# Four of seven Strassen products in two matmuls where a call also has plain units, with tighter room for prefetch and folded scales

## The chip, the cores and the metric

The kernel runs on one core of a Trainium2 chip. The metric is the device time of one execution in microseconds (us), as the median of several runs. Beside it stands one profiled execution, from which every duration below is read. "PE" is TensorE's matmul stream, "PEld" its weight loads (which overlap it), "DVE" VectorE, "ACT" ScalarE, "POOL" GpSimd and "SP" SyncE, which here only issues DMAs.

## The reference

One layer of a decoder trunk over 512 tokens with width 2048, all in float32:

```python
h = rmsnorm(x, attn_norm_g)
u, v_sgu, q, k, v_att, g_a, g_b = split(h @ w_in)          # 2048 -> 9216 columns
y_a = gelu(u) * chunked_spatial_gating(rmsnorm(gelu(v_sgu)))  # 8 groups, chunks of 128
y_b = stick_breaking_attention(rmsnorm(q, q_norm_g), rmsnorm(k, k_norm_g), v_att)  # 8 heads of 128
merged = sigmoid(g_a) * (y_a @ w_up_a) + sigmoid(g_b) * (y_b @ w_up_b)
x = x + merged @ w_o
hid = rmsnorm(x, ffn_norm_g) @ w_ffn_in                    # 2048 -> 2 x 5632
x = x + (silu(gate) * up) @ w_ffn_out                      # 5632 -> 2048
x = x + sigmoid(rmsnorm(x, ple_norm_g) @ w_ple_gate) * (p @ w_ple)
```

The attention's scores are scaled by 1/sqrt(128). All RMS norms add 1e-6 to the mean square.

## The kernel before

**Numbers in two halves.** A float32 value is split into a high half, rounded to the type that the matmul takes at full rate (fp32r), and a low half, the rest. A product of two such values needs high x high, high x low and low x high. `mm3` (lines 275 to 279) issues these as three matmuls: the high weight against the high data, the high weight against the low data, the low weight against the high data. The high half is made by an ACT copy, the low half by a DVE subtraction: `split_into` (L272, L273) for the data, `Weights.steps` (L346, L343) for the weights. A split operand is called a form; its halves lie in the arena `parts`, its raw block in the arena `wholes`.

**Units and calls.** One unit is a 256 x 256 block of a weight against 256 rows and 512 tokens of data. A call (`pair`) makes 256 output columns for all tokens and goes over the units of the inner dimension. A unit is either plain ("P": four block products, each an `mm3` over 512 tokens) or Strassen ("S", in Winograd's form: seven products of 128 x 128 blocks against 256 columns, for which sums of data blocks and of weight blocks are prepared). Two neighbouring units of one kind share one weight transfer and are worked product by product together. The strings `OUT`, `PASSES` and `GATE` tell the kinds: w_o and the gate have "SSSSSSPP", FFN-out goes in three passes over its inner dimension with "SSSSSSPP", "SSSSSSP" and "SSSPPPP". The calls of w_in and FFN-in are all "S".

**Single and doubled products.** The data's high and low halves lie side by side. A doubled product (`twice`, L686) therefore runs the high weight once over 512 columns, high and low halves together, into a whole PSUM bank, and the low weight over 256 columns into that bank's first half: two matmuls and two weight loads in place of three, with the same 768 columns. The two halves of the bank have to be added later. The number of doubled products of a call is its argument `doubled`: five in w_in, seven in FFN-in. Where a call has plain units too, the kernel before sets it to zero, and all seven products go through `mm3`.

**Banks and mixing.** There are six rotating PSUM banks ("ps") and two more ("small"). An undoubled call holds four banks: "a" and "q" (two products each in halves), "z" and "y". With plain units, these run into z and y as well. While the last Strassen units run, `mix` takes one step after each product: ACT copies a and q out (L697), DVE adds them up (L700). At the end `rest` subtracts from y and adds to z on DVE (L779). `mix_doubled` (L729, L732) does the like for the all-Strassen calls, with each doubled bank's first half copied by ACT and its second half added by DVE.

**Order.** The program text is written by Python, and a scheduler orders each engine's instructions; `in_turn` and `tick` tie some of them to places among the units. A tick comes about once a plain unit and twice a pair of Strassen units. At a tick the first form waiting in `builds` is made if its room can be had, one of the first three is fetched, and sums of late forms are made. A late form is one whose raw block is fetched ahead of its place in `parts`; its four sums (`sums_of`, L531) go into two extra blocks. Whether room can be had is asked by `fits` (L163 on), which tries the takes, a spare block of 1024 that the caller adds, and one more of 1024 that it adds itself. `keep_for` decides at the end of a call whether the block just finished is kept as the next form's raw block. In w_o, the next layer's forms may be fetched from the second last call on.

**Queues.** SP issues nearly all transfers, in one order: weights (L326, L328, L330), blocks of x, of the hidden layer and of partial sums (L513), and stores. POOL issues the weight sums, which add in flight (L350). At the start SP issues both halves of p, then the weight of the first product (`w_ple[0]`, L326), then x and the gains (L887); five small matmuls on zeros run ahead (L881). The squares of x for the first norm are made as each block of x is scaled (`norm1.add`, L935, L939).

**Scales.** q is multiplied by its RMS factor and, in a DVE operation on that factor (L1052), by 1/sqrt(128), then by its gain on ACT while it is copied out (L1057). k is multiplied by its gain in an ACT pass of its own over 1024 columns (L1065).

## Time and profile before

| | us |
|---|---|
| median of 3 runs | 2702.89 (2701.41 to 2705.18) |
| profiled execution | 2700.52 |
| its span, first to last instruction | 2698.7 |
| PE busy | 2664.3 |
| PEld busy | 2369.2 |
| DVE busy | 2201.6 |
| ACT busy | 1368.7 |
| POOL busy | 388.7 |

The granted TensorE clock is 0.997 of full speed over the span. 536.20 MB move over the DMA queues, 199 GB/s in the mean. Busy times are unions over the span and overlap each other; a matmul's row covers its way through the array, so neighbouring matmuls overlap too, and the rate of the stream is read from starts or from the length of a stretch and the count in it. L-numbers are lines of the kernel before. By the rows of the trace, w_in and its attention run to about 845 us, the two up-projections to 1025, w_o to 1180, FFN-in from 1188 to 2054, the three FFN-out passes to 2534 with bounds near 2235 and 2390, and the gate to the end.

### The profile page before, as it was taken

The page shows a single profiled execution, that of the slowest core. Times are in us where ns is not written, and L with a number is a line of the kernel's source. Part 1 is how long each engine was busy: PE and PEld are TensorE (multiplying, and loading weights), DVE is VectorE, ACT ScalarE, POOL GpSimd, SP SyncE. Part 2 cuts the span into 40 slices and gives each one's busy share as a digit, 9 for nine tenths or more (in the row PEclk, how much of TensorE's full clock was granted, in tenths as well). Part 3 has the DMA queues.
Part 4 walks back from the last instruction along what each step waited for, and adds up shares of the span by engine and source line. Part 5 has one row for each costly group of instructions (what it writes and reads, how often), then busy time and mean ns, then how long its engine had stood idle before and what let it go on. Part 6 is the DMA issues. An engine that isn't in the chain of part 4 may idle for free.

```text
span 2698.7 us, 43910 instructions
## 1 busy us (share of the span) xinstructions
PE 2664.3 (99%) x16244; PEld 2369.2 (88%) x16244; DVE 2201.6 (82%) x3750; ACT 1368.7 (51%) x2143; POOL 388.7 (14%) x450
## 2 busy tenths in 40 slices
PE   9999999999999999999999999999999999999999
PEld 7888888888988889988888888888888999989898
DVE  7787878787887668788999898989899668788876
ACT  7655656565554334465444444444445344444643
POOL 0212121212220001101111111111110101101010
PEclk9999999999999999999999999999999999999999
DMA  6676677767776458767887878877877768878784
GB/s 214 168 181 167 177 177 177 178 175 193 175 186 213 133 151 251 208 204 194 222 212 196 208 201 202 205 203 196 213 196 214 188 175 248 229 246 242 251 251 128
DMA packets 287879, 536.20 MB, mean 199 GB/s; under 512 B 25648, under 2 KB 140720, under 8 KB 287664
## 3 DMA queue, kind: packets, MB, share of 16 engines
q1 hardware_dynamic: 228016, 426.55, 49.5%
q0 software_dynamic: 59648, 106.85, 24.0%
q8 instruction: 127, 2.08, 0.3%
q14 instruction: 88, 0.72, 0.1%
HBM read 486.11 MB, written 47.19 MB: 198 GB/s over the span
## 4 chain that ended last, share of the span: by engine, by line
PE 82%; DVE 9%; DMA 3%; ACT 3%; issue 2%; POOL 1%; SPq 0%; DVEq 0%; ACTq 0%; POOLq 0%
PE ps L686 37%; PE ps L279 13%; PE ps L277 13%; PE ps L278 13%; PE small L686 4%; DVE wlo L343 3%; DVE out L732 1%; DVE parts L273 1%; ACT whi L346 1%; DMA wholes<-w_in 1%; DVE wholes L531 1%; DVE wholes L732 1%; DMA wholes<-x 1%; PE small L1126 1%; PE small L1084 1%
## 5 line engine op out<-in xcount | busy, mean ns | idle before, releaser
L346 ACT ACTIVATE whi<-wholes 128x512 fp32r<-128x512 f32 (+3 forms) x937 | 854.9, 938 | 834.2 <-PE ps L278 318.3
L686 PE MATMUL ps<-parts,whi 128*128 128x512 f32 x3384 | 1129.3, 398 | 4.2 <-DVE p L732 2.9
L343 DVE TENSOR_TENSOR wlo<-wholes,whi 128x512 fp32r<-128x512 f32 (+3 forms) x937 | 972.8, 1072 | 63.6 <-ACT whi L346 61.6
L277 PE MATMUL ps<-parts,whi 128*128 128x256 f32 (+1 forms) x2784 | 869.5, 315 | 8.9 <-ACT whi L346 4.1
L278 PE MATMUL ps<-parts,whi 128*128 128x256 f32 (+1 forms) x2749 | 869.5, 317 | 2.9 <-DVE parts L273 2.9
L279 PE MATMUL ps<-parts,wlo 128*128 128x256 f32 (+1 forms) x2749 | 867.4, 317 | 1.7 <-DVE wlo L343 1.7
L686 PEld LDWEIGHTS ps<-parts,wlo 128*128 128x128 f32 x3384 | 635.8, 188 | 142.3 <-DVE wlo L343 1.2
L686 PE MATMUL ps<-parts,wlo 128*128 128x256 f32 x3384 | 668.3, 279 | 0.8 <-DVE wlo L343 0.8
L277 PEld LDWEIGHTS ps<-parts,whi 128*128 128x128 f32 x2784 | 529.7, 190 | 49.4 <-ACT whi L346 7.1
L278 PEld LDWEIGHTS ps<-parts,whi 128*128 128x128 f32 x2749 | 523.3, 190 | 40.3 <-DVE parts L273 3.5
L279 PEld LDWEIGHTS ps<-parts,wlo 128*128 128x128 f32 x2749 | 523.3, 190 | 35.5 <-DVE wlo L343 3.0
L686 PEld LDWEIGHTS ps<-parts,whi 128*128 128x128 f32 x3384 | 543.8, 189 | 12.1 <-DVE p L732 4.4
L362 DVE TENSOR_TENSOR wholes<-wholes 128x256 f32<-128x256 f32 (+1 forms) x810 | 339.6, 419 | 35.4 <-issue 11.8
L350 POOL DMA_DIRECT2D wholes<-w_ffn_in x172 | 147.8, 859 | 740.1 <-DMA wholes<-w_ffn_in 209.1
L732 DVE TENSOR_TENSOR out<-out,ps 128x256 f32<-128x256 f32 x373 | 152.1, 419 | 124.9 <-ACT out L729 114.9
L350 POOL DMA_DIRECT2D wholes<-w_in x132 | 115.7, 876 | 596.6 <-DMA wholes<-w_in 195.0
L273 DVE TENSOR_TENSOR parts<-wholes,parts 128x1024 fp32r<-128x1024 f32 (+4 forms) x142 | 130.3, 932 | 10.2 <-ACT parts L272 10.0
L686 PE MATMUL small<-parts,whi 128*128 128x512 f32 x344 | 136.0, 395 | 0.0
L272 ACT ACTIVATE parts<-wholes 128x1024 fp32r<-128x1024 f32 (+4 forms) x142 | 111.8, 821 | 34.8 <-DMA wholes<-hid 13.5
L1403 ACT ACTIVATE out<-out 128x512 f32<-128x512 f32 x44 | 27.9, 633 | 190.0 <-DVE out L1402 190.0
L350 POOL DMA_DIRECT2D wholes<-w_ffn_out x56 | 50.9, 908 | 403.3 <-DMA wholes<-w_ffn_out 119.5
L700 DVE TENSOR_TENSOR out<-out 128x256 f32<-128x256 f32 x36 | 15.2, 424 | 102.5 <-ACT out L697 99.1
(129 smaller groups left out, 1673.5 us busy)
## 6 DMA issues: line engine op xcount, KB each, us to landing
wholes<-w_ffn_in SPq DMA_DIRECT2D x172, 384.0 KB, 5.6
wholes<-w_in SPq DMA_DIRECT2D x132, 384.0 KB, 5.1
wholes<-w_ffn_in SPq DMA_DIRECT2D x172, 256.0 KB, 4.8
wholes<-w_ffn_in POOLq DMA_DIRECT2D x172, 256.0 KB, 5.5
wholes<-w_in SPq DMA_DIRECT2D x132, 256.0 KB, 4.2
wholes<-w_in POOLq DMA_DIRECT2D x132, 256.0 KB, 4.9
wholes<-w_ffn_out SPq DMA_DIRECT2D x49, 384.0 KB, 4.9
wholes<-x SPq DMA_DIRECT2D x32, 512.0 KB, 5.9
```

The source lines that it names most:

```text
L272: return (nc.scalar.activation(hi, src, AF.Copy), nc.vector.tensor_tensor(out=lo, in0=src, in1=hi.bitcast(F32), op=ALU.subtract))
L273: nc.vector.tensor_tensor(out=lo, in0=src, in1=hi.bitcast(F32), op=ALU.subtract))
L277: nc.tensor.matmul(ps[:, s], sh, mh[:, s], start=start, stop=False)
L278: nc.tensor.matmul(ps, sh, ml, start=False, stop=False)
L279: return nc.tensor.matmul(ps, sl, mh, start=False, stop=stop)
L343: in_turn(nc.vector.tensor_tensor(out=self.lo[:, blocks], in0=r, in1=h.bitcast(F32), op=ALU.subtract))
L346: in_turn(nc.scalar.activation(h, r, AF.Copy))
L350: nc.gpsimd.dma_start(out=raw[:, 3:5], in_=self.src[:, 1:3], accum_op=ALU.add)
L362: in_turn(nc.vector.tensor_tensor(out=o, in0=x, in1=y, op=ALU.add))
L686: i = nc.tensor.matmul(out, w, t, start=first and k == 0, stop=last and k == 1)
L732: in_turn(nc.vector.tensor_tensor(out=out, in0=x, in1=y, op=op))
L1403: nc.scalar.activation(g, g, AF.Silu)
```

## The change

1. **Four doubled products beside plain units.** `Pair.doubled` is no longer set to zero when a call has plain units, but at most four there. The first four products (P1, P6, P7, P5) go through `twice` into a bank each, the other three through `mm3` into z and y, which the plain units share. A new `mix_some` replaces `mix` in these calls. The calls that ask for it: w_o except its last two, FFN-out's first two passes except their first call (which is plain throughout) and their last, and the gate's all-but-first, 25 calls in all.
2. **Room.** `fits` no longer adds a block of its own. The spare blocks that callers add are counted from what a stage still has to load (`need`, `hold`, `release`) and are none in FFN-in and in FFN-out's first pass, one in w_o and the second pass, up to two in the third. A fetch asks for the sums of the first waiting form (`sums_ahead`), and so does `keep_for`; sums ask for their own room alone; the first form that is fetched but has not landed holds back the sums of those behind it. The sums' blocks are taken when a form is begun. FFN-in's forms may be fetched from the fourth last call of w_o on (`AHEAD`). `wholes` grows from 13200 to 13312 columns; a scratch tile of 128 columns moves into it, the first norm's accumulator also holds its row afterwards, and the third norm's accumulator is taken a pass later.
3. **Start.** The first weight comes in two transfers, one ahead of p and one behind; its splits go half by half. The gains are issued by POOL ahead of this. The squares of x for the first norm come two ticks later, and of the plain copies of x's blocks two in advance are made at two places, not at one.
4. **Scales.** 1/sqrt(128) is folded into q's RMS factor (a factor of 128 on the mean square and on epsilon), and k's gain into q's, as one column `g_qk`.

```diff
-            self.doubled = 0 if self.n["P"] else doubled
+            self.doubled = min(doubled, 4) if self.both else doubled
...
-                mix = (self.mix_doubled if self.doubled else self.mix)(self.o)
+                mix = (self.mix if not self.doubled else self.mix_some if self.both
+                       else self.mix_doubled)(self.o)
...
-                    elif self.doubled:
+                    elif self.doubled and not self.both:
...
+        def mix_some(self, o):
+
+            p1, p6, p7, p5 = [(b[:, :256], b[:, 256:]) for b in map(self.at, range(4))]
+            b = o.rearrange("p (b c) -> p b c", c=256)
+            s = tmp.tile([P, T], F32, tag="p75", name=nm("p75"), bufs=1)
+            s7, s5 = s[:, :256], s[:, 256:]
+
+            def whole(out, x, scale=1.0):
+                in_turn(nc.scalar.activation(out, x[0], AF.Copy, scale=scale))
+                tt(out, out, x[1], ALU.subtract if scale < 0 else ALU.add)
...
+            whole(b[:, 0], p1, -1.0)
+            yield
+            whole(b[:, 1], p6, -1.0)
+            yield
+            whole(s7, p7)
+            tt(b[:, 1], b[:, 0], b[:, 1])
+            yield
+            whole(s5, p5)
+            tt(b[:, 2], b[:, 1], s7)
+            yield
+            tt(b[:, 1:4:2], b[:, 1:3], s5.unsqueeze(1).to_broadcast([P, 2, 256]))
+            yield
...
-            for arena, n, how in sizes + [(wholes, 1024, "low")]:
+            for arena, n, how in sizes + spare_blocks():
...
-                if fits([(wholes, f.fetches, "low")] + spare_blocks()):
+                if fits([(wholes, f.fetches, "low")] + sums_ahead()):
...
+    def sums_ahead():
+        return SUMS * any(f.late and f.sums is None for f in list(builds)[:1])
...
     def spare_blocks():
-        return [(wholes, 1024, "low")] * spared[0]
+        return [(wholes, 1024, "low")] * max(0, needed[0] - held[0])
...
-            elif fits(SUMS + spare_blocks()):
+            elif fits(SUMS):
...
+    gcol = consts.tile([P, ng], F32, name="gcol")
+    nc.gpsimd.dma_start(out=gcol, in_=gains)
+    w = plain_weights(w_ple[0], True)
     ple_operands()
-    ple_pair(0, False)
+    w.load_half(1)
+    ple_pair(0, False, w)
...
-            norm1.add(x_raw[k])
-            give(x_raw[k])
+
+            def add(b=x_raw[k]):
+                norm1.add(b)
+                give(b)
+
+            after(2, add)
...
-            token_rms(ps, r)
-            nc.vector.tensor_scalar(out=r, in0=r, scalar1=float(P) ** -0.5, scalar2=None,
-                                    op0=ALU.mult)
+            token_rms(ps, r, float(P))
...
-            nc.scalar.activation(s, flip(qn), AF.Copy, scale=gcol[:, g_q : g_q + 1])
+            nc.scalar.activation(s, flip(qn), AF.Copy, scale=g_qk)
...
-        nc.scalar.activation(o, o, AF.Copy, scale=gcol[:, g_k : g_k + 1])
...
-        if j == KU - 2:
+        if j == KU - AHEAD:
             for f in fs:
                 f.early = True
-        pr = pair(ms, last=j == KU - 1)
+        pr = pair(ms, last=j == KU - 1, doubled=4 if j < KU - 2 else 0)
...
-            pr = pair(units, last=j == KU - 1, plain=j == 0, at=first)
+            pr = pair(units, last=j == KU - 1, plain=j == 0, at=first,
+                      doubled=4 if c < 2 and j < KU - 1 else 0)
...
-            pair(gs, parts_done=finish)
+            pair(gs, parts_done=finish, doubled=4)
         else:
-            o = pair(gs, plain=j == 0).out()
+            o = pair(gs, plain=j == 0, doubled=4).out()
```

More of the change, by code (lines that the diff above doesn't have):

```diff
@@ L324, in __init__ @@
             raw = self.blocks(self.land.f())
-            if kind == "P":
+            if halves:
+                self.load_half(0)
+            elif kind == "P":
                 nc.sync.dma_start(out=raw, in_=src)
@@ L330, in __init__, with load_half @@
                 nc.sync.dma_start(out=raw[:, 0:3], in_=src[:, 1:4])
+        def load_half(self, i):
+            b = slice(2 * i, 2 * i + 2)
+            nc.sync.dma_start(out=self.blocks(self.land.f())[:, b], in_=self.src[:, b])
         def blocks(self, t, c=None):
@@ L355, in high @@
                                     for t in self.slot)
-                split(False, slice(0, c), raw)
+                for b in (slice(0, 2), slice(2, 4)) if self.halves else (slice(0, c),):
+                    split(False, b, raw[:, b])
             def sums():
@@ L365, in rest @@
             def rest():
-                split(True, slice(0, c), raw)
+                for b in (slice(0, 2), slice(2, 4)) if self.halves else (slice(0, c),):
+                    split(True, b, raw[:, b])
                 if self.kind == "S":
@@ L462, in sum_early @@
         def sum_early(self):
-            if not self.late or self.sums or self.since is None or clock[0] < self.since + LANDS:
+            if not self.late or self.sums:
                 return False
+            if self.since is None or clock[0] < self.since + LANDS:
+                return True
             if self.gain:
                 self.scale()
-            elif fits(SUMS + spare_blocks()):
+            elif fits(SUMS):
                 self.sums = sums_of(self.raw)
@@ L521, in hybrid_layer, with sums_room, sums_of @@
     SUMS = [(wholes, 768, "tight"), (wholes, 256, "tight")]
-    def sums_of(raw):
-        b, s, v = cut(raw.f()), *(take(n, how) for _, n, how in SUMS)
+    def sums_room():
+        return tuple(take(n, how) for _, n, how in SUMS)
+    def sums_of(raw, room=None):
+        b, (s, v) = cut(raw.f()), room or sums_room()
         t = cut(s.f())
@@ L532, in sums_of, with plain_first @@
         return s, v
-    def plain_first(form, raw):
-        s, v = form.sums or sums_of(raw)
+    def plain_first(form, raw, room=None):
+        s, v = form.sums or sums_of(raw, room)
         b, t, x = cut(raw.f()), cut(s.f()), form.operand()
@@ L556, in steps @@
             form.blocks = (parts.take(2 * PLACE, "place"),)
+            room = None if form.sums else sums_room()
             if not form.sums:
@@ L559, in steps @@
                 yield
-            yield from plain_first(form, w)
+            yield from plain_first(form, w, room)
             return form.operand()
@@ L949, in steps @@
                                  start=True, stop=True)
-            give(self.acc)
             yield
@@ L967, in steps @@
             yield
-            self.block = take(T)
+            self.block = self.acc
             nc.scalar.activation(self.block.f(), ps, AF.Copy)
@@ L1022, in squares @@
     def squares(ps):
-        ms, junk = small(NT), tmp.tile([P, P], F32, tag="sq", name=nm("sq"), bufs=1)
+        ms, junk = small(NT), a_tile("j", P)
         for t in range(NT):
@@ L1277, in hybrid_layer @@
             row1 = norm1.row()
-            nc.vector.tensor_scalar(out=eps_cols, in0=norm1.mean, scalar1=EPS, scalar2=None,
-                                    op0=ALU.mult)
+            for at, e in ((0, EPS), (NT, P * EPS)):
+                nc.vector.tensor_scalar(out=eps_cols[:, at : at + NT], in0=norm1.mean,
+                                        scalar1=e, scalar2=None, op0=ALU.mult)
+            nc.vector.tensor_tensor(out=g_qk, in0=gcol[:, g_q : g_q + 1],
+                                    in1=gcol[:, g_k : g_k + 1], op=ALU.mult)
         if n == 0:
@@ L1361, in keep_for @@
         if (j < KU - KEPT or form.raw or late and late[0] is not form
-                or not fits([(wholes, 1024, "low")] * 2)):
+                or not fits(sums_ahead())):
             give(block)
@@ L1368, in hybrid_layer @@
     raw = deque()
+    need(1)
     for j in range(KU):
-        after(3, lambda j=j: raw.append(load(xT[j])))
+        after(3, lambda j=j: raw.append(hold(load(xT[j]))))
         if j == 1:
```

65 lines of the change are left out of this document (40 added, 25 removed).

## The prediction

> **What bounds the kernel now.** I read the page first, then a table of stages, then the waits of the PE alone.
>
> ```profile
> span 2698.7 us, 43910 instructions
> PE 2664.3 (99%) x16244; PEld 2369.2 (88%) x16244; DVE 2201.6 (82%) x3750; ACT 1368.7 (51%) x2143; POOL 388.7 (14%) x450
> PE 82%; DVE 9%; DMA 3%; ACT 3%; issue 2%; POOL 1%; SPq 0%; DVEq 0%; ACTq 0%; POOLq 0%
> ```
>
> PE is busy 99% of the span and is 82% of the chain that ended last. Two things can shorten the kernel: a faster stream on PE, or the few places where it waits. The table of stages gives the price of the stream (columns: length, then busy time and count for PE, weight loads, DVE, ACT, POOL, then clock, DMA share, GB/s):
>
> ```profile
> core 0: us, PE busy (x) PEld busy (x) DVE busy (x) ACT busy (x) POOL busy (x), PEclk, DMA share, GB/s
> 2101.91:2117.02 15.11, 15.11 (x128) 15.11 (x126) 7.53 (x10) 6.44 (x8) 1.70 (x2) 1.00 0.73 195
> 1240.30:2040.70 800.40, 800.22 (x4594) 697.90 (x4593) 725.47 (x1322) 377.02 (x534) 139.43 (x163) 1.00 0.81 204
> ...
> 1030.00:1176.00 146.00, 146.00 (x1060) 138.78 (x1059) 110.71 (x164) 71.17 (x87) 15.61 (x18) 1.00 0.72 199
> 1176.00:1222.00 46.00, 42.48 (x197) 35.08 (x196) 39.49 (x67) 33.71 (x51) 6.45 (x7) 0.96 0.90 266
> 2066.00:2100.00 34.00, 31.27 (x190) 27.94 (x190) 29.43 (x46) 15.48 (x22) 4.30 (x5) 0.95 0.79 228
> 2100.00:2203.00 103.00, 103.00 (x757) 98.29 (x756) 62.16 (x90) 38.75 (x45) 12.02 (x14) 1.00 0.69 185
> 2570.00:2690.00 120.00, 120.00 (x888) 114.79 (x887) 87.72 (x116) 47.38 (x54) 12.17 (x14) 1.00 0.69 193
> ```
>
> The first row is the Strassen part of one call in FFN-out: six units of seven products of three 256-column matmuls, 126 in all, in 15.11 us, or 0.3598 us a product (w_o and the gate run the same code). The second row is 41 calls of FFN-in, 41 x 8 x 7 = 2296 products of two matmuls (one of 512 columns, one of 256), in 800.4 us, or 0.3486 us a product. In the three-matmul stream PEld is full from end to end (15.11 of 15.11): a weight load goes with every 256 columns. In the rows of w_o (1030 to 1176), FFN-out (2100 to 2203, five calls of 20.6) and the gate (2570 to 2690) PE has no gap at all. What it waits for elsewhere (total, times, longest):
>
> ```profile
> PE ps L277 <- ACT whi L346: 4.1, 6, 1.3
> PE ps L277 <- ACT parts L272: 3.1, 2, 2.1
> PE ps L686 <- DVE p L732: 2.9, 4, 1.0
> PE ps L278 <- DVE parts L273: 2.9, 2, 2.0
> PE small L1114 <- DVE sp L273: 2.5, 1, 2.5
> PE small L1019 <- ACT sq L1026: 2.2, 3, 0.8
> PE ps L279 <- DVE wlo L343: 1.7, 2, 1.0
> PE small L948 <- DVE wholes L939: 1.3, 1, 1.3
> ```
>
> These are 20.7 us, small and scattered: the start, the attention of round 0, and the hand-over from one layer to the next, where the forms of the next operand (L272, L273) come late.
>
> **The change part by part.** *Four of seven doubled.* It reaches six calls of w_o, six each in two FFN-out passes, seven in the gate: 25 calls, each six Strassen units of four products, 600 products. Each goes from three matmuls to two: 600 x (0.3598 - 0.3486) = **-6.7 us**. It lies wholly on the path, as PE has no gap there.
>
> The Trainium skill, "TensorE: Matmul & The Clock Gate", section "Wait — 56ns, not 53.3ns?", puts the fixed cost of a matmul at about 2.5 ns beside its columns. By it a removed instruction would bring 600 x 2.5 ns = 1.5 us, an estimate from that page. The two rows above measure 11.2 ns in this stream, and the sum goes by them; the page's value is a rival below.
>
> The call's output is paid for by more mixing. Rows by shape (busy, mean ns, idle before):
>
> ```profile
> L729 ACT ACTIVATE out<-ps 128x256 f32<-128x256 f32 x198 | 71.0, 381 | 13.4 <-PE ps L686 13.0
> L732 DVE TENSOR_TENSOR out<-out,ps 128x256 f32<-128x256 f32 x373 | 152.1, 419 | 124.9 <-ACT out L729 114.9
> L697 ACT ACTIVATE out<-ps 128x512 f32<-128x512 f32 x36 | 21.3, 592 | 23.3 <-PE ps L279 23.3
> L531 DVE TENSOR_TENSOR wholes<-wholes 128x256 f32<-128x256 f32 x156 | 60.4, 416 | 7.6 <-ACT wholes L517 6.7 <-DMA x<-wholes 0.8
> ```
>
> Before, a call copies two banks of 512 on ACT (2 x 0.592) and adds from there. After, it copies four halves (4 x 0.381) and adds the other halves from PSUM (4 x 0.419); the three later adds stay. So ACT gets 0.34 us more a call, DVE 1.68 us, 25 x 1.68 = 42 us of DVE in all. Cover: DVE is busy 110.71 of 146 in w_o, 62.16 of 103 in FFN-out, 87.72 of 120 in the gate, so 1.68 us in a call of 20.6 lifts the fullest from 76% to 84%, still under FFN-in's 725.47 of 800.4 (91%), which mixes seven doubled products a call with PE full. The adds wait for ACT, ACT for PE; behind them in DVE's order stand the low halves of the next weights (L343), for which PE's third matmul waits. Without cover the cost is the 42 us.
>
> The new call also holds all six rotating PSUM banks (four for the doubled products, two that the plain units share), where the old one held four. The next call's fifth product now goes into the bank that the last add of this call reads:
>
> ```profile
> 2121.37 0.68 DVE L779 TENSOR_TENSOR out<-ps,out 128x512 f32<-128x512 f32 x1
> 2122.72 0.69 DVE L779 TENSOR_TENSOR out<-ps,out 128x512 f32<-128x512 f32 x1 [0.66 <-PE ps L279]
> ```
>
> The call ends at about 2122.5; that add is done at 2123.41. The next call writes the bank after eight doubled products, 8 x 0.348 = 2.8 us in, at 2125.3: a slack of 1.9 us, and DVE sat idle for 0.66 us ahead of the add. I bound the cost of both by 0 and by the longest wait of the same kind, a PE wait for a mixing add (L686 <- L732, 1.0 us), in all 25 calls: 25 us. As DVE comes early here I take a value near the low end, **+0.9 us**: one such wait.
>
> *The start.* The weight of the first product comes in halves, one ahead of the two halves of p; gains go from SP's queue to POOL's; the squares of x's norm come two ticks later.
>
> ```profile
> 3.75 1.27 ACT L272 ACTIVATE parts<-wholes 128x512 fp32r<-128x512 f32 x2 [1.66 <-DMA wholes<-pT]
> 6.09 0.63 ACT L346 ACTIVATE whi<-wholes 128x512 fp32r<-128x512 f32 x1 [1.07 <-DMA wholes<-w_ple]
> 22.77 2.00 ACT L935 ACTIVATE out<-wholes 128x1024 f32<-128x1024 f32 x2 [0.43 <-DMA ple<-out]
> 24.68 0.61 ACT L346 ACTIVATE whi<-wholes 128x512 fp32r<-128x512 f32 x1
> 6.77 0.50 PE L277 MATMUL ps<-parts,whi 128*128 128x512 f32 x1 [1.00 <-ACT whi L346]
> 25.35 0.50 PE L277 MATMUL ps<-parts,whi 128*128 128x512 f32 x1 [1.28 <-ACT whi L346]
> ```
>
> ACT idles 1.07 us until the weight lands, and PE starts 0.68 us after ACT does. With the first half landed beside p (p about 0.4 us later, by one issue ahead of it), ACT's splits of p end at 4.15 + 1.27 = 5.4, and the half weight's (256 columns, 0.381 as in L729) at 5.8, where PE can start: -0.9. At 22.77 two squares (2.00 us) stand ahead of the high half that PE waits 1.28 us for; moved back, they leave that wait. Bounds: nothing, since ACT must still do the squares in this phase and may be late one unit on, and the 4.1 + 0.7 us of waits for weights (L346, and the earlier of L343's two). I take **-1.9**, those two less 0.3 that comes back. Gains on POOL stand ahead of making the identity, which nothing needs so soon.
>
> *Scales.* Folded: a 4-column multiply for each half of q (its eight rows are DVE's L1052), and the pass of k's gain over 1024 columns, merged into q's.
>
> ```profile
> L1065 ACT ACTIVATE wholes<-wholes,gcol x4: 1142/1147/1147, 106.8 to 523.3; 128x1024 f32<-128x1024 f32 x4
> ACT wholes L1041 <- DVE rr L1052: 21.4, 7, 5.5
> ```
>
> It frees 4 x 1.147 us of ACT and up to 21.4 us of ACT idling for a hop through DVE. PE does not wait for k's gain by name; it waits in this stage for squares and a low half (2.2 + 2.5 us). Bounds 0 and 4.7; **-0.4**, near the low end since ACT is half idle and neither wait names the removed operations.
>
> *Room.* The try for room asks for what is still to be loaded instead of a fixed spare block and another, and asks for the sums of the first late form with each fetch; forms of FFN-in may come from the fourth last call of w_o on, not the second last. So more raw blocks and sums lie ready at a hand-over.
>
> ```profile
> 1198.62 0.49 SPq L513 DMA_DIRECT2D wholes<-x  x1
> 1206.65 1.34 ACT L517 ACTIVATE wholes<-wholes,gcol 128x512 f32<-128x512 f32 x2 [2.59 <-DMA wholes<-x]
> 1210.15 1.00 PE L277 MATMUL ps<-parts,whi 128*128 128x512 f32 x2 [2.08 <-ACT parts L272]
> 2072.67 0.50 PE L278 MATMUL ps<-parts,whi 128*128 128x512 f32 x1 [1.99 <-DVE parts L273]
> 2074.30 0.63 PE L279 MATMUL ps<-parts,wlo 128*128 128x512 f32 x1
> 2076.86 0.63 PE L279 MATMUL ps<-parts,wlo 128*128 128x512 f32 x1
> ```
>
> At 1207 the last x block is issued at 1198.62, for want of room, and PE waits 2.08 us at the end of that line. At 2070 DVE is full (29.43 of 34 us) with sums: 4 x 0.416 = 1.7 us a form. After each the clock drops (0.96 and 0.95 in the stages' rows): seven matmuls from 2074.30 on start 0.427 us apart (2.56/6), where two thirds of FFN-in's 0.3486, or 0.232, is usual: 7 x 0.19 = 1.3 us more. Bounds: nothing, and all waits of the hand-overs, 3.1 + 2.9 + 1.3 + 1.0 plus two slow spells of 1.3, 10.9 us; a loss of one such wait with its spell, 3.4, when a block taken too early holds SP's queue. Each sum moved ahead frees 1.7 us on the full engine, so I take **-3.7**, one of the two long waits with its spell and a little.
>
> Sum: -6.7 + 0.9 - 1.9 - 0.4 - 3.7 = **-11.8 us**. The profiled execution took 2700.5 us (1.8 around its span), so 2688.7; the median of the runs is 2.4 above it, so **2691**.
>
> **The rivals.** *Doubling alone*: hand-overs and start give nothing, as ACT and DVE stay as full there; -6.7 + 0.9 gives 2697.1. For it: the deferred work is still to be done in the same stage. Against: the waits stand behind named work that is moved away.
>
> *The columns set the rate*: a product streams 768 columns before and after, and FFN-in's lower price may come from its neighbours (seven doubled in a row, two units back to back on one weight order), not from the missing instruction. Then doubling gives nothing, and 0.9 - 1.9 - 0.4 - 3.7 = -5.1 leaves 2697.8. Against: PEld, full in the old stream, is at 697.90 of 800.4 in FFN-in. The page's 2.5 ns stand for most of this rival; by them the time would be 2696.3.
>
> *The gain is eaten*: a block taken too early costs a new wait with its spell, 3.4 us, and the other waits stay: -6.7 + 0.9 + 3.4 = -2.4, 2700.5. For it: SP's queue already issues the last x late. Against: the try asks for everything that the next load needs.
>
> *The shared bank*, the other side: DVE does the last add behind a form's four sums (1.7 us) and a low half, later than the 1.9 us of slack, and every call waits at its fifth product. From 11.8/25 = 0.5 us a call on the whole gain is gone; at 1.0 us, the longest wait for a mixing add, 25 - 11.8 gives +13, 2716. For it: L686 does wait so elsewhere. Against: DVE's idle time before L779.
>
> **How the numbers follow.** Chances: the forecast 0.66, doubling alone 0.14, the columns 0.04, eaten 0.08, the bank 0.08. A measurement of this kernel can tell about 0.2%, 5.4 us, from no change, so faster is below 2697.5. The forecast counts as faster, and of doubling alone, which lies on that line, 0.10: 0.76. Its other 0.04 with the columns and the eaten gain are the same, 0.16; the bank is slower, 0.08. The likeliest one's own range is 2684 (all of the start's and the scales' bounds, 4.8 and 4.7, are worth 7.2 more than I took) to 2697; the range for 8 in 10 runs on to the eaten gain, 2684 to 2702.
>
> **What would show it.** Calls of w_o, FFN-out passes 0 and 1 and the gate 0.27 us shorter (24 x 0.0112) with PE full; no wait of PE for L779; the first weighted matmul at about 5.8 and no wait at 25; the long waits at the ends of w_o and FFN-in halved and the clock there nearer 1.00. Waits of about 1 us at the fifth product of calls would show the shared bank. The prediction is wrong if the doubled products cost 0.36 us, or if hand-overs get new waits of 2 us.

## The result, and the profile after

The changed kernel takes 2689.71 us in the median of four runs (2687.82 to 2690.58); the kernel before, timed beside it, takes 2704.03 (2701.41 to 2705.53). The ratio is 0.9948, with a 95% interval of 0.9935 to 0.9960. A second set (seven runs against 21, below) gives 0.9964 (0.9951 to 0.9977). The forecast was 2691 and faster. What follows shows that the total came out for reasons which are only partly those of the forecast.

The page of the profiled execution (2690.24 us), span, busy times and the chain of the changed kernel:

```profile
span 2688.4 us, 42845 instructions
PE 2661.0 (99%) x15644; PEld 2338.4 (87%) x15644; DVE 2232.7 (83%) x3845; ACT 1371.2 (51%) x2190; POOL 390.9 (15%) x451
PE 83%; DVE 9%; ACT 3%; DMA 2%; issue 2%; POOL 1%; SPq 0%; DVEq 0%; ACTq 0%; POOLq 0%
```

PE has 600 matmuls less (15644 for 16244), DVE 31.1 us more. The stages of the changed kernel, columns as before; the first row is the Strassen part of one call in FFN-out, the same six units that took 15.11 us:

```profile
2095.60:2110.43 14.83, 14.83 (x103) 13.62 (x102) 10.52 (x20) 6.71 (x10) 1.73 (x2) 1.00 0.81 214
1030.00:1176.00 146.00, 144.20 (x921) 131.31 (x920) 119.22 (x191) 76.31 (x104) 14.57 (x17) 0.99 0.74 206
1176.00:1222.00 46.00, 44.16 (x212) 36.82 (x211) 36.36 (x61) 32.00 (x47) 7.18 (x8) 0.96 0.89 260
```

The call is 0.28 us shorter, and PE and the clock are full in it. In w_o, which had no gap, PE now has one of 1.8 us, and in the last row the clock is 0.96 as before. What PE waits for (total, times, longest) in the changed kernel, by its own line numbers:

```profile
PE small L1009 <- DVE wholes L1000: 2.6, 1, 2.6
PE ps L292 <- ACT whi L368: 2.5, 4, 0.9
PE ps L293 <- DVE parts L288: 2.4, 2, 2.3
PE small L1148 <- ACT wholes L1108: 1.9, 1, 1.9
PE ps L292 <- ACT out L918: 1.8, 1, 1.8
PE ps L292 <- DVE out L838: 1.8, 1, 1.8
```

The wait for ACT's split of the data (L272 before, 3.1 us) is gone and the one for weights is down from 4.1 to 2.5. But one has come, 1.8 us for the last add of a w_o call (L838, the old L779), and one has grown, from 1.3 to 2.6 us, for the third norm's sums (L1009 on L1000, the old L948 on L939) at the hand-over to the gate.

**Place in the column stream.** The kernels stream the same 5,725,464 columns through PE. For a time in the profile of before I count the columns begun by then, and find when another kernel has begun as many: the difference is its lead. The table has how the lead changes over stretches of before's time (us; negative is gained). The heads name what each kernel has of the change; they are told below. Each column comes from one profiled execution, so a step counts where several kernels repeat it.

```
stretch        after   arena  doubl.   start,  start,   all but   all but  all but
                       alone  alone    scales  scales   the room  doubl.   the start
                                       +arena  no arena
                        (e9)    (e2)    (e5)    (e8)     (e4)      (e1)     (e3)
   0 to   60    -3.7     1.4     2.3    -2.4    -2.9      -3.3      -2.9      2.3
  60 to  140     1.2     0.3    -2.2     1.6     4.0       0.1       1.0     -3.3
 140 to 1050    -3.1    -0.4     1.0     1.4    -2.4       3.2       3.2     -0.2
1050 to 1175     2.7     0.0    -1.1     0.0     0.0      -1.1       0.0      0.8
1175 to 1215    -1.4    -3.1    -2.2    -2.5     1.6      -4.0      -1.7     -1.8
1215 to 2100    -2.0    -2.7    -1.1    -1.0    -2.1      -2.3      -3.4     -1.6
2100 to 2230    -1.4     0.0    -1.5     0.0     0.0      -1.5       0.0     -1.4
2230 to 2260    -2.4    -0.9     2.3    -1.2     0.5       0.9      -2.4     -2.5
2260 to 2375    -1.1    -0.2    -1.7    -0.2    -0.2      -1.7      -0.2     -1.1
2375 to 2405    -1.3    -1.3     0.3    -1.3     1.6      -1.3      -1.3     -1.3
2405 to 2550     4.6     1.2     2.2     1.2     0.5       0.6       4.0      4.8
2550 to 2691    -2.4    -0.4    -1.8    -0.4     0.5      -2.3      -0.4     -2.4
all            -10.2    -6.2    -3.4    -4.8     1.0     -12.8      -4.0     -7.5
```

Inside calls (2100 to 2230, 2260 to 2375, 2550 on) only the doubled kernels gain, each by about the same. At hand-overs the kernels differ in both directions, and there most of the case is decided. How far one execution can be trusted is seen from a second one of the changed kernel (below): at 1050 to 1175 it loses 1.2 us where the table has 2.7, and at 2405 to 2550 it loses 2.3 where the table has 4.6.

### The profile page after: what moved, and what is told of

The parts are those of the page before. It is cut to its first block, busy times and chain, and to the rows that moved or that the text cites. A ratio compares the mean times of both kernels' runs of the same rounds, so it can differ in the third digit from the quotient of the medians.

```text
span 2688.4 us, 42845 instructions
## 1 busy us (share of the span) xinstructions
PE 2661.0 (99%) x15644; PEld 2338.4 (87%) x15644; DVE 2232.7 (83%) x3845; ACT 1371.2 (51%) x2190; POOL 390.9 (15%) x451
## 4 chain that ended last, share of the span: by engine, by line
PE 83%; DVE 9%; ACT 3%; DMA 2%; issue 2%; POOL 1%; SPq 0%; DVEq 0%; ACTq 0%; POOLq 0%
PE ps L716 45%; PE ps L292 11%; PE ps L293 11%; PE ps L294 10%; PE small L716 4%; DVE wlo L365 3%; DVE parts L288 1%; ACT whi L368 1%; DVE out L791 1%; DVE wholes L791 1%; DVE wholes L385 1%; DMA wholes<-xT 1%; PE small L1190 1%; PE small L1148 1%; DVE wholes L559 1%
## 5 line engine op out<-in xcount | busy, mean ns | idle before, releaser
L716 PE MATMUL ps<-parts,whi 128*128 128x512 f32 x3984 | 1330.0, 398 | 2.9 <-DVE out L791 1.8
L368 ACT ACTIVATE whi<-wholes 128x512 fp32r<-128x512 f32 (+4 forms) x938 | 855.7, 938 | 837.9 <-DVE wholes L385 347.6
L365 DVE TENSOR_TENSOR wlo<-wholes,whi 128x512 fp32r<-128x512 f32 (+4 forms) x938 | 972.7, 1071 | 83.9 <-ACT whi L368 78.2
L716 PE MATMUL ps<-parts,wlo 128*128 128x256 f32 x3984 | 787.1, 279 | 0.0
L292 PE MATMUL ps<-parts,whi 128*128 128x256 f32 (+1 forms) x2184 | 702.2, 324 | 7.0 <-ACT whi L368 2.5
L293 PE MATMUL ps<-parts,whi 128*128 128x256 f32 (+1 forms) x2149 | 701.1, 326 | 2.4 <-DVE parts L288 2.4
L294 PE MATMUL ps<-parts,wlo 128*128 128x256 f32 (+1 forms) x2149 | 701.1, 326 | 0.5 <-DVE wlo L365 0.3
L716 PEld LDWEIGHTS ps<-parts,whi 128*128 128x128 f32 x3984 | 642.3, 189 | 11.1 <-issue 4.8
L292 PEld LDWEIGHTS ps<-parts,whi 128*128 128x128 f32 x2184 | 414.9, 190 | 46.7 <-ACT whi L368 3.9
L293 PEld LDWEIGHTS ps<-parts,whi 128*128 128x128 f32 x2149 | 408.3, 190 | 43.3 <-DVE parts L288 3.9
L788 ACT ACTIVATE out<-ps 128x256 f32<-128x256 f32 x198 | 70.9, 380 | 14.0 <-PE ps L716 13.8
```

Source lines behind the costliest of these rows:

```text
L292: nc.tensor.matmul(ps[:, s], sh, mh[:, s], start=start, stop=False)
L293: nc.tensor.matmul(ps, sh, ml, start=False, stop=False)
L294: return nc.tensor.matmul(ps, sl, mh, start=False, stop=stop)
L365: in_turn(nc.vector.tensor_tensor(out=self.lo[:, blocks], in0=r, in1=h.bitcast(F32), op=ALU.subtract))
L368: in_turn(nc.scalar.activation(h, r, AF.Copy))
L716: i = nc.tensor.matmul(out, w, t, start=first and k == 0, stop=last and k == 1)
```

## The experiments

The theory was the sum of the prediction: doubling 5.8 (6.7 less 0.9), room 3.7, start 1.9, scales 0.4. Its rivals here: the parts do not add up, since what one gains the next hand-over takes back; or the gain comes from an edit that the sum left out. Every time is a median with its range; ratios are to the kernel before on the same chip, with 95% intervals; 0.001 is 2.7 us.

**Taking parts away (before: 2701.98, 28 runs).** Without doubling, where a call has plain units:

```diff
-        pr = pair(ms, last=j == KU - 1, doubled=4 if j < KU - 2 else 0)
+        pr = pair(ms, last=j == KU - 1)
...
-            pair(gs, parts_done=finish, doubled=4)
+            pair(gs, parts_done=finish)
```

> The changed kernel with no doubled product beside plain units; room, start and scales as changed. Instruction theory: each of the 600 products costs 11 ns more again, +6.7 us, less one PE wait of 2.0 us in w_o's second call that the doubling brought (with a slow spell of about 0.6), so about 2694 where the changed kernel takes 2689.7; the calls of FFN-out's first two passes and of the gate are 0.27 us longer. Rival, the columns set the rate: about 2690 or less, calls of equal length.

Measured 2696.22 (2691.77 to 2701.72, 12 runs), ratio 0.9978 (0.9968 to 0.9987): 5.9 us gained. The changed kernel's two sets average 0.9956, so on top of the rest doubling is worth about 0.0022, 5.9 us, where 5.8 was forecast. When the intervals are put together, the 5.9 has an uncertainty of some 3.5.

The kernel before with doubling and nothing else (the line of `Pair.doubled`, `mix_some` and the arguments of the diff):

```diff
-            self.doubled = 0 if self.n["P"] else doubled
+            self.doubled = min(doubled, 4) if self.both else doubled
```

> The kernel before with the doubling alone. Instruction theory: -6.7 us, plus what the shared banks cost: 0 to 2.6 us (one wait with its spell), so 2697 to 2700 where the kernel before takes 2704. Columns theory: 2704 or a little more. Shared-bank theory: over 2704, with waits of PE for the last adds in most calls.

Measured 2701.26 (2696.98 to 2705.61, 12 runs), ratio 1.0001 (0.9991 to 1.0011): nothing. Yet its trace has the whole gain inside the calls (-1.5, -1.7 and -1.8 in the three stretches). It loses 2.3 us at the hand-over from the first FFN-out pass to the second and 2.2 us at the one to the gate. Its waits of PE:

```profile
PE ps L278 <- DVE parts L273: 4.7, 3, 2.6
PE ps L277 <- ACT whi L346: 4.3, 4, 2.1
PE ps L277 <- ACT parts L272: 2.8, 2, 1.5
```

The wait for DVE's half of the next form (L273) is 4.7 us where it was 2.9; at the first of those two hand-overs it is 1.6 where it was 0.9: PE comes sooner to a hand-over where DVE is late already. At the gate the norm's wait is 1.4 as against 1.3, and the loss there is mostly a stretch of 3.4 us with the clock at 0.50 (2534.0 to 2537.4; 1.00 in the kernel before). So the gain is real in the call. That it is given back at hand-overs which DVE ends is seen at one of them; for the whole it is the reading that fits the ratio, and is not shown wait by wait.

The changed kernel with the start of before:

```diff
-    gcol = consts.tile([P, ng], F32, name="gcol")
-    nc.gpsimd.dma_start(out=gcol, in_=gains)
-    w = plain_weights(w_ple[0], True)
     ple_operands()
-    w.load_half(1)
-    ple_pair(0, False, w)
+    ple_pair(0, False)
     load_x()
+    gcol = consts.tile([P, ng], F32, name="gcol")
+    nc.sync.dma_start(out=gcol, in_=gains)
...
-            after(2, add)
+            add()
```

> The changed kernel with the old start (whole first weight behind p, gains on SP, squares of x at once, copies of x's blocks two ahead at one place). My forecast had the start at 1.9 us: 2691.6. By the place in the column stream the changed kernel was 3.7 us ahead at 60 us but only 0.4 us at 100 us: if that is a debt paid back within the stage, this kernel takes 2690 to 2690.5, PE's waits coming back near 24 us and those near 63 to 83 us going.

Measured 2689.82 (2687.49 to 2692.89, 6 runs), ratio 0.9956 (0.9942 to 0.9969): the start's gain cannot be seen, though 1.9 us is less than these intervals can tell. By the table the kernels with the new start are 2.4 to 3.7 us ahead at 60 us, and those with the old one behind; at 140 the lead is 2.4 us with the new start (the changed kernel) and 1.0 with the old.

The changed kernel with the try for room as it was (spare blocks as in the kernel before, `fits` adding its own, `AHEAD` of 2, the third norm's accumulator taken early); the arena keeps its 13312 columns:

```diff
-            for arena, n, how in sizes + spare_blocks():
+            for arena, n, how in sizes + [(wholes, 1024, "low")]:
...
-                if fits([(wholes, f.fetches, "low")] + sums_ahead()):
+                if fits([(wholes, f.fetches, "low")] + spare_blocks()):
...
-        return [(wholes, 1024, "low")] * max(0, needed[0] - held[0])
+        return [(wholes, 1024, "low")] * spared[0]
...
-AHEAD = 4
+AHEAD = 2
```

> The changed kernel with the old try for room (a spare block and another, fetches and sums each with a spare, w_o's last two calls alone fetch for FFN-in, third norm's accumulator early). My forecast had the room at 3.7 us: 2693.4. By the place in the column stream the five hand-overs give -2.4, -0.9, -2.4, -1.3 and +4.6, together -2.4: 2692. Rival, room gives nothing: 2689.7, with the same waits at the hand-overs.

Measured 2692.94 (2687.53 to 2697.97, 11 runs), ratio 0.9965 (0.9954 to 0.9976), against 0.9948 and 0.9964 with the new try. The try itself is worth nothing that can be told. In the table the new one is better by 3.3 us at 2230 to 2260 (-2.4 for 0.9), and worse by 2.6 us at 1175 to 1215 and by 4.0 at 2405 to 2550 (by 1.7 in the second execution of the changed kernel). (The steps ahead of 1175 differ by 6.3 one way and by 3.8 the other, and I read nothing from them.)

**What is left, and the two waits (before: 2700.82, 21 runs).** The changed kernel again, unedited:

> The changed kernel once more, on the chip of the three runs beside it, to have one base for all of them: 2688 to 2691 where the kernel before takes 2702 to 2704.

Measured 2692.27 (2689.99 to 2695.29, 7 runs), ratio 0.9964 (0.9951 to 0.9977), 9.7 us.

Doubling and room both undone (the diffs of the first and fourth experiment together), so that start, scales and the arena's size are left:

> The changed kernel with both the doubling and the room undone: start and scales alone. With the run without doubling (-5.8 us against the kernel before), the one with the old room (-9) and the changed kernel (-14) it fills a square. If doubling and room add up, it is at 5.8 + 9 - 14, -1 us, about 2702. If each is worth most only with the other (hand-overs are bound by VectorE, so a faster PE waits there for longer until the room moves sums ahead), it is below what the sum says: at -3 to -5, 2698. My forecast for start and scales was -2.3.

Measured 2695.58 (2692.02 to 2697.77, 9 runs), ratio 0.9976 (0.9965 to 0.9986): 6.5 us, where start and scales were put at 2.3. In its column of the table the gain is not at the start: it stands at 1175 to 1215, 2230 to 2260 and 2375 to 2405, hand-overs that neither edit touches. What else was left in it is the arena `wholes`, 13312 columns where it had 13200. 13312 is 13 blocks of 1024; 13200 holds twelve and 912 columns over. That became the new theory. This kernel prices the two larger parts a second time. The fourth experiment has the doubling beside it and else the same: 0.0011, 3.0 us, with an uncertainty of some 4. The first has the new try for room beside it and else the same: 0.9978 for 0.9976, nothing.

The waits of PE in w_o and at the gate, with p's splits in w_o six ticks later and the third norm's chain two later:

```diff
+        def splits():
+            for s in halves:
+                split_into(hi.own()[:, s], lo.own()[:, s], raw.f()[:, s])
+            give(raw)
...
-            ple_operands()
+            ple_operands(6)
...
-    after(3, norm3.chain.step)
+    after(5, norm3.chain.step)
```

> The changed kernel with two waits of PE aimed at. In w_o's second call the splits of p come six ticks after its transfer is issued, so that ScalarE doesn't sit 4 us before p lands with a mixing copy behind it: if that was what made the last adds late, PE's wait of 1.8 us for the shared bank and its slow spell go (-2.5 us). The third norm starts two ticks later, so that its first matmuls don't wait 2.6 us for the last add of squares: that wait and its slow spell of eleven matmuls and more go (-4.5 us). Both together 2683 where the changed kernel takes 2689.7. Rival for the bank: VectorE is late from its own load; then the wait stays. Rival for the norm: the row comes later and the first gate call's finish holds a bank; then a new wait of 1 to 3 us comes near 2550.

Measured 2691.56 (2687.00 to 2693.41, 6 runs), ratio 0.9958 (0.9943 to 0.9972). The time is no other than the unedited kernel's as far as can be told. The wait of 1.8 us in w_o is gone and with it that stretch's loss (1050 to 1100: 0.0 for +3.1). The 3.1 are that wait and 3.4 us with the clock at 0.50 behind it (1049.2 to 1052.6); the second execution of the changed kernel has the wait (1.7) without the slow clock and loses 1.5. In the changed kernel's timeline the wait had come about so (start, length, engine, work, and the idle time ahead with its releaser):

```profile
1034.38 0.33 SPq L901 DMA_DIRECT2D wholes<-pT  x1
1039.42 0.63 ACT L287 ACTIVATE parts<-wholes 128x512 fp32r<-128x512 f32 x1 [3.97 <-DMA wholes<-pT]
1039.96 0.37 ACT L757 ACTIVATE p<-ps 128x256 f32<-128x256 f32 x1
1041.03 2.09 DVE L365 TENSOR_TENSOR wlo<-wholes,whi 128x1280 fp32r<-128x1280 f32 x2
1045.22 2.08 DVE L365 TENSOR_TENSOR wlo<-wholes,whi 128x1280 fp32r<-128x1280 f32 x2
1047.22 0.68 DVE L838 TENSOR_TENSOR out<-ps,out 128x512 f32<-128x512 f32 x1
1047.96 0.39 PE L292 MATMUL ps<-parts,whi 128*128 128x256 f32 x1 [1.80 <-DVE out L838]
```

ACT stood 3.97 us on p's transfer with the mixing's copy behind it; DVE's adds came late, low halves of weights were worked ahead of the last add, and PE waited for the shared bank. The norm's wait did not go, it is 3.0 us: its matmuls stand at the same place in PE's order.

Twice the mixing's load on DVE: four more adds of 256 columns in each doubled call, whose results are overwritten (25 x 4 x 0.42 = 42 us):

```diff
             whole(b[:, 0], p1, -1.0)
+            tt(s5, b[:, 0], b[:, 0])
...
             whole(s7, p7)
+            tt(s5, s7, s7)
+            tt(s5, s7, s7)
```

> The changed kernel with four more adds of 256 columns on VectorE in each doubled call, into scratch: the extra load of mixing twice, 25 x 1.68 = 42 us more. If the calls cover it as I forecast, the time is the same within 1 us, 2690 to 2691. If mixing delays the work for the next weights or the last adds, calls get waits: +5 us and more, up to +42. If only the hand-overs, which VectorE bounds, pay: +2 to +4, with longer waits for the forms at the ends of w_o and FFN-out's first passes.

Measured 2695.74 (2692.89 to 2699.41, 12 runs), ratio 0.9980 (0.9970 to 0.9990), 0.0016 or 4.3 us above the unedited kernel, with an uncertainty of some 4 when the two intervals are put together. Its first wait of PE is one that the changed kernel has not by name:

```profile
PE ps L716 <- DVE wlo L365: 3.4, 7, 1.4
PE ps L292 <- ACT out L922: 3.2, 2, 2.1
```

The seven waits of the first line stand in w_o and in FFN-out's second pass, in calls that mix. So DVE's cover looks not quite free: of a second 42 us about a tenth comes through, at the edge of what the times can tell, as low halves of weights that are late. It says nothing of the first 42 us by itself.

**The arena (before: 2702.28, 15 runs).** Start and scales as above, now with the arena of before:

```diff
-WHOLES = 13312
+WHOLES = 13200
```

> Start and scales alone (doubling and room undone, as in the run that came out 6.5 us under the kernel before), now also with the arena back at 13200 columns. In that run the place in the column stream showed nothing gained up to 1026 us and 4.8 us gained at the hand-overs, which neither the start nor the scales touch. Arena theory: 13312 is 13 whole blocks of 1024 and 13200 is not, the hand-overs gain from the thirteenth; then this kernel is within 2 us of the kernel before. Rival, the scales and the start bring it: -5 to -7 again.

Measured 2700.07 (2696.76 to 2702.73, 11 runs), ratio 0.9989 (0.9980 to 0.9998), for 0.9976 with the larger arena. It is 3.0 us (0.5 to 5.4) under the kernel before, where start and scales were put at 2.3. By times alone the 3.5 us between the two kernels are just at the edge of what can be told; the traces are plainer. They differ in that number alone, and the three hand-overs go from -2.5, -1.2 and -1.3 to +1.6, +0.5 and +1.6.

The other way about: the kernel before with the larger arena alone, the squares' scratch of 128 columns moved into it as in the change, so that it fits:

```diff
-WHOLES = 13200
+WHOLES = 13312
...
-        ms, junk = small(NT), tmp.tile([P, P], F32, tag="sq", name=nm("sq"), bufs=1)
+        ms, junk = small(NT), a_tile("j", P)
```

> The kernel before with one thing changed: the arena at 13312 columns, the scratch of 128 columns moved into it. Arena theory: -4 to -6 us, about 2697, with PE's place in the column stream unchanged up to 1026 us and 2 to 3 us ahead from 1215, more from 2260 and 2405 on. Rival: no change, within 2 us.

Measured 2691.87 (2689.94 to 2694.49, 5 runs), ratio 0.9959 (0.9946 to 0.9971): 11.1 us (7.8 to 14.6), as much as the whole change, where 4 to 6 were expected. That is far from the 3.5 of the pair ahead. By the table the two pairs agree: from 1175 us on the larger arena gains 7.4 us here and 7.8 there (5.4 gained for 2.4 lost). So I take some 7 us as its worth, and the 11.1 of five runs as the high end. The scratch is moved in both kernels of that pair, so it is not what separates them. The mechanism can be read at the end of w_o. The fetches of the last two x blocks and PE's wait in this kernel:

```profile
1179.50 0.33 SPq L513 DMA_DIRECT2D wholes<-x  x1
1190.03 0.46 SPq L513 DMA_DIRECT2D wholes<-x  x1
1212.26 0.71 PE L966 MATMUL small<-out,ones 128*128 128x128 f32 x4 [0.40 <-DVE out L922]
1176.00:1222.00 46.00, 44.58 (x216) 37.08 (x215) 42.88 (x74) 36.33 (x54) 11.61 (x8) 1.00 0.91 271
```

In the kernel before the last block was issued at 1198.62, and PE waited 2.08 us for its split at 1210. Here it is issued at 1190.03, 8.6 us sooner, that wait is gone, and the clock stays at 1.00 where it was 0.96. The experiment ahead of this one, without and with the larger arena, has the same fetch at 1197.98 and 1189.97; first the one with the old arena:

```profile
1182.66 0.34 SPq L536 DMA_DIRECT2D wholes<-x  x1
1197.98 0.46 SPq L536 DMA_DIRECT2D wholes<-x  x1
1210.32 0.73 PE L292 MATMUL ps<-parts,whi 128*128 128x512 f32 x2 [1.34 <-ACT parts L287]
1214.07 0.50 PE L293 MATMUL ps<-parts,whi 128*128 128x512 f32 x1 [1.39 <-DVE parts L288]
```

and with the larger one:

```profile
1178.87 0.33 SPq L536 DMA_DIRECT2D wholes<-x  x1
1189.97 0.45 SPq L536 DMA_DIRECT2D wholes<-x  x1
```

112 columns let one raw block more be in the arena, and the last form of a hand-over is ready. A count of the kernel's takes says the same for this place: at the end of w_o, 5632 columns are held for weights (512, and four times 1280) and 512 for a norm, which leaves 7056 of 13200, at most six blocks of 1024, and 7168 of 13312, seven. That the size acts by this count is argued; no run has tried a size in between. Nor has a run the new try for room with the old arena: in the changed kernel the last block is issued at 1172.93, sooner still, so the try might have removed that wait by itself.

**Mending the hand-over to the gate.** The changed kernel waits there for the third norm, and its timeline shows what was late:

```profile
2497.39 0.42 SPq L538 DMA_DIRECT2D wholes<-x  x1
2511.19 0.33 SPq L538 DMA_DIRECT2D wholes<-x  x1
2518.09 1.34 ACT L542 ACTIVATE wholes<-wholes,gcol 128x512 f32<-128x512 f32 x2 [6.53 <-DMA wholes<-x]
2522.75 1.22 DVE L1521 TENSOR_TENSOR wholes<-wholes 128x1024 f32<-128x1024 f32 x1
2522.86 0.33 SPq L538 DMA_DIRECT2D wholes<-x  x1
2526.82 0.68 DVE L1000 TENSOR_TENSOR wholes<-wholes,out 128x512 f32<-128x512 f32 x1
2527.56 1.86 PE L1009 MATMUL small<-ones,wholes 128*128 128x1 f32 x8 [2.64 <-DVE wholes L1000]
```

ACT stands 6.53 us at the gain of an x block that was issued at 2511.19, and the last sum of x and the norm's adds come behind it. Between 2498 and 2522 SP issues one block of x. So does the kernel before, at 2509.86, but PE comes to this place 12.5 us later in it. With the old try for room (fourth experiment) it issues four in that time:

```profile
2498.95 0.43 SPq L536 DMA_DIRECT2D wholes<-x  x1
2504.65 0.32 SPq L536 DMA_DIRECT2D wholes<-x  x1
2510.27 0.33 SPq L536 DMA_DIRECT2D wholes<-x  x1
2518.33 0.42 SPq L536 DMA_DIRECT2D wholes<-x  x1
```

So I gave the last pass one spare block more (with p's splits later, as above), and in a second kernel w_o too, with `AHEAD` of 2:

```diff
-        need(c)
+        need(c + (c == len(PASSES) - 1))
...
-                    need(0)
+                    need(1)
```

> The changed kernel with p's later splits and, in FFN-out's last pass and the gate, one spare block of 1024 more in the try for room, as before the change. The tighter try began forms there as soon as their block was asked for, so that ScalarE sat 6.5 us before it landed and the squares of the third norm came late. Theory: the 3 to 5 us lost at the hand-over to the gate (2520 to 2550) go, and the 1.5 to 3 us lost at w_o's second call: 2684 to 2686 where the changed kernel takes 2690 to 2692. Rival: the loss at the gate comes from the earlier arrival of PE and stays: 2688 to 2691.

Measured 2690.89 (2690.26 to 2692.05, 5 runs), ratio 0.9955 (0.9942 to 0.9967). The stretch to the gate still loses 5.5 us (2520 to 2550), as the rival had it. Blocks now come at 2501.35, 2503.62 and 2509.24 and the norm's wait is gone from the list, but another stands in its place:

```profile
2527.32 0.50 PE L293 MATMUL ps<-parts,whi 128*128 128x512 f32 x1 [3.01 <-DMA x<-wholes]
```

The second kernel:

```diff
-    need(1)
+    need(2)
...
-AHEAD = 4
+AHEAD = 2
```

> The run before it, with one spare block more in w_o too and FFN-in's forms fetched from the second last call of w_o on, as before the change. Kernels with the old try gained 2.2 to 4.0 us between 1175 and 1215 us, those with the new one 1.2 to 1.8: 1 to 2 us more than the run before it, 2683 to 2685. Rival: no difference between the two.

Measured 2689.41 (2686.32 to 2693.90, 5 runs), ratio 0.9951 (0.9938 to 0.9964). The hand-over at the end of w_o gains 3.0 us as the old try does (1175 to 1215), the one to the gate still loses 3.2 (2520 to 2550). Both forecasts were missed. The interval covers the changed kernel's: no version here is shown to beat it.

## Why the prediction was right or wrong

*Four of seven doubled, price in the call: right.* 0.0112 us a product was forecast from two different stages; the Strassen part went from 15.11 to 14.83, 0.0117 for each of its 24 products. The rival that the columns set the rate is out. The Trainium skill, "TensorE: Matmul & The Clock Gate", section "Wait — 56ns, not 53.3ns?", has about 2.5 ns of fixed cost for a matmul; the trace shows 11.7 ns for one removed from this stream, and the measurement decides. A weight load goes with each here: PEld, busy 15.11 of 15.11 us before, is at 13.62 of 14.83.

*"It lies wholly on the path, as PE has no gap there": the step that failed in this part.* There is no gap in those calls, but behind every few calls stands a hand-over, and what the calls gain is not kept through it as a matter of course. Doubling alone gains some 5 us in the calls and has a ratio of 1.0001. On top of the larger arena it is worth 5.9 us by one pair of kernels and 3.0 by another. The rival "doubling alone" (2697.1) had the right picture and the wrong price: it kept the whole 6.7 - 0.9.

*Mixing and the shared bank, +0.9: too low, and not in its place.* The slack of 1.9 us at L779 holds in FFN-out and the gate, where no such wait appears. One wait of 1.8 us came in w_o and cost 1.5 to 3.1 us in two executions; there "DVE comes early here" fails, as ACT stood behind p's transfer. I had costed the bank from one FFN-out call, without asking what stands ahead of the mixing on ACT in other stages. The rival (25 such waits, 2716) is out.

*The start, -1.9: the steps right, the sum not told.* The first weighted matmul begins at 5.01 (5.8 forecast, 6.77 before), the wait at 25 is gone, and the lead at 60 us is 3.7. By 100 us the lead is 0.4: between 60 and 100 PE waits 1.9 us for high halves of weights, where it waited 0.4 before. At 140 the lead is 2.4, and 1.0 with the old start; by times that kernel is not slower. So more than the 0.3 of the sum comes back at once; whether 1.9 is left at the end is under what the runs can tell. The part's bound was read too high: of the 4.1 us of waits for high halves, 0.7 stands at the end of FFN-in and 0.4 behind 60 us.

*Scales, -0.4:* not tried by themselves; start and scales together, with the arena of before, have 3.0 us (0.5 to 5.4) for the 2.3 forecast. The lead's steps from 140 to 1050 scatter from -3.1 to +3.2 among the kernels with folded scales (the two without have -0.4 and 1.0), so nothing can be read at that size.

*Room, -3.7: the gain came, from an edit that I did not cost.* The prediction put it on the try for room: "more raw blocks and sums lie ready at a hand-over". That picture is right, and the 2.08 us wait at 1210 and its slow spell do go (in the changed kernel another spell stands at 1182, so that the clock of that stretch is no nearer to 1.00). But what brings it is the arena of 13 x 1024 columns, which the change lists in half a sentence and no step of the sum has. By times it brings 11.1 us (7.8 to 14.6) to the kernel before and 3.5 to another, by the column stream some 7: about twice the 3.7 of the part, within its bound of 10.9. The try for room nets nothing beside it in either pair: better between the FFN-out passes, worse at the gate. What it would bring with the old arena was not run. The long wait at the end of FFN-in (1.99) did not halve either; it is 2.26 in the changed kernel.

*The gain eaten* had its mechanism at the gate: blocks held back, though, not taken too early, a wait of 2.6 us with its spell, 4.6 us lost in that stretch (1.7 in the second execution, where the wait is 2.1 and the clock stays at 1.00). It did not decide the sum, since the arena had brought more.

That the total came out is luck in good part: doubling has about its price, but the other half, which the sum gave to room, start and scales, comes from a term that it does not have, by the column stream wholly, by one pair of times for half of it. What stays open: why, by times, start, scales and arena together (6.5 us, 3.8 to 9.5) bring no more than the arena alone (7.8 to 14.6); the intervals touch, and no run separates them. Open too is what holds the gate back with a spare block more, and which block the 112 columns make room for in the later hand-overs.

## What to carry to other kernels

A faster stream on the bounding engine is kept only up to the next hand-over that another engine ends, so an edit is to be priced both alone and on top of the others: here the same doubling brought nothing alone, and 3.0 and 5.9 us on top of other edits. Divide what is left of every pool by the size of the blocks that are taken from it before anything else: 112 columns, under 1% of an arena, were worth some 7 us, and as much as the whole change by one pair of times. And compare kernels by their place in a common stream of work, since steps that repeat from kernel to kernel stand out there when whole times scatter by some us.

## What the runs showed of the hardware beyond this

The clock can fall after a wait of some 2 us, and need not. The changed kernel at the end of FFN-in and at the gate (start and length of matmuls of 512 columns, then the granted clock of two stretches):

```profile
2066.08 0.60 PE L293 MATMUL ps<-parts,whi 128*128 128x512 f32 x1 [2.26 <-DVE parts L288]
2066.48 0.63 PE L294 MATMUL ps<-parts,wlo 128*128 128x512 f32 x1
2066.91 0.63 PE L292 MATMUL ps<-parts,whi 128*128 128x512 f32 x1
...
2069.47 0.53 PE L293 MATMUL ps<-parts,whi 128*128 128x512 f32 x1
2063.00:2075.00 12.00, 9.74 (x36) 7.58 (x35) 12.00 (x21) 4.91 (x7) 0.00 (x0) 0.86 0.75 218
2529.50:2534.50 5.00, 5.00 (x13) 3.93 (x14) 4.46 (x9) 3.33 (x5) 1.19 (x1) 0.55 0.83 271
```

From 2066.48 the matmuls start 0.43 us apart where 0.23 is usual, up to 2069.47, seven of them: 1.4 us beside the wait of 2.26. The kernel with the old try for room (fourth experiment) waits 2.53 us at the same place, the one with the larger arena alone 3.20 us in the attention, and in both the clock stays:

```profile
2066.51 0.50 PE L293 MATMUL ps<-parts,whi 128*128 128x512 f32 x1 [2.53 <-DVE parts L288]
2066.84 0.39 PE L294 MATMUL ps<-parts,wlo 128*128 128x512 f32 x1
2067.07 0.40 PE L292 MATMUL ps<-parts,whi 128*128 128x512 f32 x1
2063.00:2075.00 12.00, 9.47 (x43) 7.57 (x42) 12.00 (x20) 5.49 (x9) 0.00 (x0) 1.00 0.76 222
128.19 0.33 PE L1115 MATMUL small<-sp,tri 128*128 128x128 f32 x1 [3.20 <-DVE sp L273]
122.00:134.00 12.00, 8.80 (x53) 7.34 (x52) 7.67 (x19) 7.78 (x20) 2.82 (x3) 1.00 0.69 164
```

And shorter waits have a slow stretch behind them in the changed kernel: the clock is 0.50 from 1049.2 to 1052.6, after 1.80 us, and from 1182.3 to 1185.7, after 1.84. So the length of a wait does not settle it, and what does is not shown here. Such a stretch of 3.4 us at half the clock costs some 1.7 us, by which two executions of one kernel can differ at the same wait. The Trainium skill, "TensorE: Matmul & The Clock Gate", section "HAM oscillation — how this bites in real kernels", gives the rule that PE should have no idle gaps above some 3.4 us; here the clock fell after 1.80 to 2.64 us and did not after 2.53 and 3.20, and the measurement decides.

The kernel before itself spreads over 2696.15 to 2710.05 in 64 runs, so that one profiled execution can stand some 6 us off another of the same kernel: of doubling alone the profiled run was its fastest (2696.98), of the arena alone its slowest (2694.49), so that by these single runs the arena is worth 2.5 us more than doubling, and by the medians 9.4.
